# Sparse attention of a hybrid decoder block: a unit's transposes first, then its value products in one row from the last tile, with eight transposed tiles in one ring

## The chip, the cores and the metric

The kernel runs on one core of a Trainium2 chip. The metric is the device time of one execution in microseconds (us). Five engines of the core work side by side, each through its own instructions in a fixed order: TensorE (PE in the profile; PEld are its weight loads), VectorE (DVE), ScalarE (ACT), GpSimd (POOL), and SyncE (SP), which here issues all DMAs. Matrix results land in PSUM, eight banks of 512 float32 columns on 128 partitions; ScalarE and VectorE copy from there to SBUF.

## What is computed

One decoder block on 1024 tokens of width 1024: RMS norm, one input projection, two groups of attention heads side by side, a gated sum, an output projection and the residual. The reference, cut to the parts that the change touches and their neighbours:

```python
o_diff = diff_attention(dq, dk, dv, lam, diff_slopes)          # 4 heads, two softmaxes each
o_cmp, p_cmp = compressed_attention(nq, kc, vc)                # 63 compressed keys
sel_idx = select_blocks(p_cmp)                                 # top 8 blocks of 64 keys
o_slc = selected_attention(nq, k_slc, nkv[3], sel_idx, nsa_slopes)
o_win = window_attention(nq, k_win, nkv[5], nsa_slopes)        # band of 512 keys
o_nsa = g[0] * o_cmp + g[1] * o_slc + g[2] * o_win
o_nsa = o_nsa.transpose(0, 3, 1, 2, 4).reshape(B, T, NSA_WIDTH) * jax.nn.silu(nz)
x = x + jnp.concatenate([o_diff, o_nsa], axis=-1) @ w_out[layer]
```

The sparse group has 8 query heads on 2 key/value heads of width 64. Everything is float32; the scores and projections use a high and a low part of their operands in float32r.

## The kernel before

Three stages follow each other. **Stage 1** makes all projections, and writes queries, keys, values and gates to DRAM. **Stage 2** is the sparse attention. It goes over eight q tiles of 128 tokens (`qt`). In each it takes branch 1 (window, at most five key tiles) and branch 0 (selected, up to `qt + 1` key tiles, the choice of blocks done as a mask), and in each branch two head pairs `gp`. One such piece, q tile by branch by `gp`, is a *unit*: 32 units in all. A unit's scores and softmax are `nsa_softmax` (which calls `softmax_pair`: scores on PE at L439, mask and row minimum on DVE at L443, exponential on ACT at L445; then POOL scales the rows at L585, in tiles called P or Pw). Its second half is `nsa_values` (L604): for each key tile, four transposes of 128x128 into one PSUM tile Tp (L611), a copy of Tp to the SBUF tile pT (`evac`: two of three on ACT at L489, the third on DVE at L487), and two value products (L615) that read pT and the values vsw and add into the accumulator O, one for each key/value head, each with 64 output columns. The products of float32 operands show as two records each, so that one key tile has four L615 records. There are 132 key tiles over all units.

Around it, in each q tile: the compressed branch of the *next* q tile (`cmp_branch`: products L516, DVE work from L519 on), its transposed weights pcT (copy L656, product L658 which starts O), and the output projection of the *previous* q tile (`out_proj`, L475 to L477, 24 matmuls of 512 columns). **Stage 3** is the differential attention, q tiles from 7 down to 0, four heads each; its transposes are at L733, its copies use the same `evac`, its value products are at L737. It reads the keys of heads 0 and 1 from dkA and of heads 2 and 3 from dkB, and the values from dv, which it loads at its beginning (L690).

What sets the order: the kernel is written for a scheduler that places each engine's instructions by its own model of time; the written order gives dependencies and priority, not the final sequence. Two PSUM tiles serve all transposes (`psT`, 2 buffers). pT has four buffers in a pool that lives for stages 2 and 3; pcT has one buffer of its own. The weights of the output projection are loaded in eight pieces `wraw` (two DMAs each in stage 2) through two buffers, and split by ACT (L461) and DVE (L463 in stage 2) into woh and wol before their first use.

Of the kernel before, what the change touches and what calls it, by code (L numbers as in the profile page):

```python
# [8 lines left out]
F32 = mybir.dt.float32  # L9
# [18 lines left out]
def block_kernel(ctx: ExitStack, tc: tile.TileContext, x, norm_g, w_in, dq_g, dk_g, lq1, lk1, lq2, lk2,  # L28
                 sub_g, nq_g, nk_g, cmp_pos, cmp_w1, cmp_b1, cmp_w2, w_out, out):
    nc = tc.nc  # L30
# [18 lines left out]
    def T_tile():  # L49
        return psT.tile([128, 512], F32, tag="T", name="Tp")  # L50

    def A_tile():
        return psA.tile([128, 512], F32, tag="A", name="A")


    ident = const.tile([128, 128], F32, name="ident")
# [107 lines left out]
    with ExitStack() as p1:  # L164
# [5 lines left out]
        st = ctxS.enter_context(tc.tile_pool(name="p1s", bufs=2))  # L170
# [73 lines left out]
        with ExitStack() as pc:  # L244
# [5 lines left out]
            for tt in range(NT):  # L250
# [8 lines left out]
                raw = st.tile([128, 512], F32, tag="qn", name="kvraw", bufs=3)  # L259
# [135 lines left out]
        sh = ctx.enter_context(tc.tile_pool(name="attn", bufs=2, side="right"))  # L395
# [48 lines left out]
                                               scalar=3e38, op0=ALU.add, op1=ALU.min, accum_out=nm)  # L444
                nc.scalar.activation(Ps[a][:, :n], Ps[a][:, :n], AF.Exp, scale=-1.0, bias=nm, accum_out=ssums[a])  # L445

        def load_w_out(pool, raws, k0):

            woh = pool.tile([128, 4, 1024], F32R, name="woh")
            wol = pool.tile([128, 4, 1024], F32R, name="wol")  # L450
            for k in range(4):
                for nh in range(2):
                    c = slice(512 * nh, 512 * nh + 512)
                    raw = raws.tile([128, 512], F32, tag="wraw", name="wraw", bufs=2)
                    if k0 == 0:
                        nc.sync.dma_start(raw, w_out[128 * k:128 * k + 128, c])
                    else:
                        for j in range(2):
                            r0 = 512 + 256 * j + 64 * k
                            nc.sync.dma_start(raw[64 * j:64 * j + 64], w_out[r0:r0 + 64, c])  # L460
                    nc.scalar.activation(woh[:, k, c], raw, AF.Copy)  # L461
                    eng = nc.vector if k0 else nc.gpsimd
                    eng.tensor_tensor(wol[:, k, c], raw, woh[:, k, c].bitcast(F32), op=ALU.subtract)  # L463
            return woh, wol
# [16 lines left out]
        evac_n = [0]  # L481

        def evac(Tp, n=512, every=3):
            pT = sh.tile([128, 512], F32, tag="pT", name="pT", bufs=4)
            evac_n[0] += 1
            if evac_n[0] % every == 0:
                nc.vector.tensor_copy(pT[:, :n], Tp[:, :n])  # L487
            else:
                nc.scalar.activation(pT[:, :n], Tp[:, :n], AF.Copy)  # L489
            return pT  # L490
# [65 lines left out]
        def nsa_span(qt, br):  # L556
            k0 = max(0, qt - 4) if br == 1 else 0
            return k0, 128 * (qt + 1 - k0)
# [44 lines left out]

        def nsa_values(qt, br, gp, Ps, O):  # L604
            k0, n = nsa_span(qt, br)
            for kt in range(n // 128):
                Tp = T_tile()
                for j in range(2):
                    for g2 in range(2):
                        c = 256 * j + 128 * g2  # L610
                        nc.tensor.transpose(Tp[:, c:c + 128], Ps[g2, j][:, 128 * kt:128 * kt + 128], ident)  # L611
                pT = evac(Tp, 512, 3)
                last = br == 0 and gp == 1 and kt == n // 128 - 1
                for j in range(2):
                    nc.tensor.matmul(O[64 * j:64 * j + 64, 256 * gp:256 * gp + 256],  # L615
                                     vsw[:, br, k0 + kt, 64 * j:64 * j + 64], pT[:, 256 * j:256 * j + 256],
                                     start=False, stop=last)

        q_first = q_stack(q_d["nq"][0])
        for m in (2, 3, 0, 1):  # L620
# [2 lines left out]
        pools, early = {}, {}  # L623
# [16 lines left out]

    with ExitStack() as p2:
        pools["w"] = p2.enter_context(tc.tile_pool(name="p2w", bufs=1))
        keep = p2.enter_context(tc.tile_pool(name="p2k", bufs=1))
        st = p2.enter_context(tc.tile_pool(name="p2s", bufs=2))
        vsw = keep.tile([128, 2, NT, 128], F32, name="vsw")
        nc.sync.dma_start(vsw, v_d)
        wo_n = load_w_out(keep, st, 4)
        pending = None
        for qt in range(NT):
            t0 = 128 * qt  # L650
            QH, QL, nzt, gate, pg, rep = nxt
            Tp = A_tile()
            for g in range(4):
                nc.tensor.transpose(Tp[:, 128 * g:128 * g + 128], pg[:, g].rearrange("p k c -> p (k c)"), ident)
            pT = pools["w"].tile([128, 512], F32, tag="pcT", name="pcT", bufs=1)
            nc.scalar.activation(pT, Tp, AF.Copy)  # L656
            O = A_tile()
            nc.tensor.matmul(O, vcbd, pT, start=True, stop=False)  # L658
            if qt + 1 < NT:
                nxt = cmp_branch(qt + 1)  # L660


            for br in (1, 0):
                for gp in range(2):
                    Ps = early.pop((qt, br, gp), None) or nsa_softmax(qt, br, gp, QH, QL, gate, rep)
                    nsa_values(qt, br, gp, Ps, O)
            if pending:
                out_proj(*pending)
            nc.vector.tensor_tensor(nzt, O.rearrange("p (g q) -> p g q", g=4), nzt, op=ALU.mult)
            ch = st.tile([128, 4, 128], F32R, tag="ch", name="ch")  # L670
            cl = st.tile([128, 4, 128], F32R, tag="cl", name="cl")
            nc.scalar.activation(ch, nzt, AF.Copy)
            nc.gpsimd.tensor_tensor(cl, nzt, ch.bitcast(F32), op=ALU.subtract)
            pending = (st, ch, cl, wo_n, x[t0:t0 + 128], xa_d[qt], 1)
        O_first = A_tile()
        out_proj(*pending)
# [4 lines left out]
    with ExitStack() as p3:  # L681
        kp = p3.enter_context(tc.tile_pool(name="p3k", bufs=1))
        p2p = p3.enter_context(tc.tile_pool(name="p3p", bufs=1))
        big = p3.enter_context(tc.tile_pool(name="p3big", bufs=1))
        st = p3.enter_context(tc.tile_pool(name="p3s", bufs=1))
        right = p3.enter_context(tc.tile_pool(name="p3r", bufs=1, side="right"))
# [4 lines left out]
        for m in range(4):  # L691
            k_load(dkB[:, m], "dk", 4 + m)
        wo_d = load_w_out(big, st, 0)

        def loads(qt):
# [16 lines left out]
        for i, qt in enumerate(order):  # L712
            t0 = 128 * qt
            n = t0 + 128
# [3 lines left out]
            O = A_tile() if i else O_first  # L718
            for h in range(4):
# [9 lines left out]
                for k4 in range(0, qt + 1, 4):  # L729
                    kn = min(4, qt + 1 - k4)  # L730
                    Tp = T_tile()
                    for k in range(kn):
                        nc.tensor.transpose(Tp[:, 128 * k:128 * k + 128], P0[:, 128 * (k4 + k):128 * (k4 + k) + 128], ident)  # L733
                    pT = evac(Tp, 128 * kn, 4 if qt > 4 else 2)
                    for k in range(kn):
                        kt = k4 + k
# [40 lines left out]
```

## Time and profile before

| | us |
|---|---|
| median of three runs (range) | 832.72 (831.93 to 833.76) |
| the profiled execution | 832.81 |
| its span, first to last instruction | 831.1 |
| PE busy in the span | 795.2 (96%) |
| DVE, ACT, POOL busy | 511.4, 368.4, 357.3 |
| first transpose of stage 2 (L611) | 399.8 |
| last value product of stage 2 (L615) starts | 686.0 |

The page gives busy times over the whole span; a window gives the same for a stretch. A timeline shows instructions in order of time, equal neighbours merged into one row with a count. The end of a matmul is a model, its start is not, so distances between starts are what a price of a matmul is read from. PEclk is the share of the full TensorE clock that was granted.

### The profile page before, as it was taken

How to read it: one execution, taken by the hardware profiler on the slowest of the kernel's cores; microseconds unless marked ns; L12 is line 12 of the kernel's file. 1: busy time of each engine (PE TensorE's matmuls, PEld its weight loads, DVE VectorE, ACT ScalarE, POOL GpSimd, SP SyncE). 2: the span in 40 equal slices, each digit the busy share in tenths (PEclk: the TensorE clock that was granted, in tenths of full speed). 3: DMA queues.
4: the chain of work that ended last, by engine and by line, in shares of the span. 5: the costliest groups of instructions: out<-in, count | busy, mean ns of one | idle time of the engine just before them, and what ended most of it. 6: DMA issues, size and time to landing. Idle time of an engine off the chain costs nothing.

```text
span 831.1 us, 12884 instructions
## 1 busy us (share of the span) xinstructions
PE 795.2 (96%) x4457; PEld 631.1 (76%) x4457; DVE 511.4 (62%) x1183; ACT 368.4 (44%) x811; POOL 357.3 (43%) x385
## 2 busy tenths in 40 slices
PE   5999799999999999999899999999999999998997
PEld 4898688888888888888666666666665658888975
DVE  4644643368634439932697577776775267989743
ACT  6543131231323232012686656564656365867510
POOL 6734262250625434040476526263443314876421
PEclk9999999999999999999999999999999999999999
DMA  8637463151434423166543232121120426533233
GB/s 283 175 75 228 124 211 107 25 154 49 140 101 119 123 44 97 50 175 167 178 115 102 77 103 74 55 64 51 50 66 1 117 63 192 164 93 111 65 127 114
DMA packets 74897, 91.99 MB, mean 111 GB/s; under 512 B 14032, under 2 KB 48976, under 8 KB 74704
## 3 DMA queue, kind: packets, MB, share of 16 engines
q1 hardware_dynamic: 74832, 91.18, 37.7%
q8 instruction: 35, 0.57, 0.3%
q14 instruction: 30, 0.25, 0.1%
HBM read 63.89 MB, written 27.26 MB: 110 GB/s over the span
## 4 chain that ended last, share of the span: by engine, by line
PE 79%; DMA 7%; DVE 6%; POOL 2%; issue 2%; ACT 2%; SPq 2%; POOLq 0%; ACTq 0%; DVEq 0%
PE S L439 10%; PE A L615 9%; PE Tp L611 9%; PE A L208 5%; PE S L210 5%; PE A L210 5%; PE A L209 5%; PE S L209 5%; PE S L208 5%; PE A L475 3%; PE A L477 3%; PE A L476 3%; PE A L737 3%; PE Tp L152 2%; DMA xt<-in_x_dram 1%
## 5 line engine op out<-in xcount | busy, mean ns | idle before, releaser
L445 ACT ACTIVATE P<-P,nm 128x128 f32<-128x128 f32 (+7 forms) x136 | 101.2, 747 | 32.9 <-DVE nm L443 29.6
L489 ACT ACTIVATE pT<-Tp 128x512 f32<-128x512 f32 (+3 forms) x118 | 67.3, 575 | 90.8 <-PE Tp L611 72.1
L135 POOL TENSOR_TENSOR r<-ss,neghalf 128x8 f32<-128x8 f32 (+2 forms) x41 | 55.9, 1364 | 119.6 <-DVE ss L133 114.6
L200 POOL TENSOR_TENSOR wlo<-raw,whi 128x512 fp32r<-128x512 f32 (+2 forms) x64 | 82.4, 1315 | 50.8 <-ACT whi L199 49.3
L208 PE MATMUL A<-whi,xh 128*128 128x512 f32 (+2 forms) x224 | 86.6, 386 | 0.0
L208 PE MATMUL S<-whi,xh 128*128 128x512 f32 (+2 forms) x224 | 86.3, 385 | 0.3 <-ACT xh L240 0.2
L210 PE MATMUL S<-whi,xl 128*128 128x512 f32 (+2 forms) x224 | 86.5, 386 | 0.0
L209 PE MATMUL S<-wlo,xh 128*128 128x512 f32 (+2 forms) x224 | 86.1, 385 | 0.0
L210 PE MATMUL A<-whi,xl 128*128 128x512 f32 (+2 forms) x224 | 85.8, 383 | 0.0
L209 PE MATMUL A<-wlo,xh 128*128 128x512 f32 (+2 forms) x224 | 85.7, 383 | 0.0
L615 PE MATMUL A<-pT,vsw 128*64 128x256 f32 x528 | 84.7, 404 | 0.8 <-DMA vsw<-v_d 0.8
L585 POOL TENSOR_SCALAR P<-P,ssum 128x128 f32<-128x128 f32 (+7 forms) x72 | 51.5, 736 | 49.5 <-DVE ssum L581 20.3
L443 DVE CUSTOM_DVE_ANT_0 P<-S,D 128x128 f32<-128x128 f32 (+7 forms) x96 | 60.7, 659 | 18.1 <-PE S L439 12.0
L439 PE MATMUL S<-nsaK,QH 128*128 128x384 f32 (+2 forms) x192 | 68.9, 366 | 2.2 <-DVE nm L443 2.2
L585 POOL TENSOR_SCALAR Pw<-Pw,ssum 128x640 f32<-128x640 f32 (+3 forms) x56 | 39.1, 718 | 61.4 <-DVE ssum L581 37.1
L439 PE MATMUL S<-nsaK,QL 128*128 128x384 f32 (+2 forms) x192 | 61.4, 334 | 0.0
L160 DVE RECIPROCAL e<-e 128x512 f32<-128x512 f32 (+1 forms) x18 | 57.1, 3174 | 0.6
L487 DVE COPY pT<-Tp 128x512 f32<-128x512 f32 (+3 forms) x62 | 38.4, 619 | 30.5 <-PE Tp L611 28.9
L475 PE MATMUL A<-woh,ch 128*128 128x512 f32 x128 | 52.3, 409 | 4.3 <-ACT ch L705 3.3
L199 ACT ACTIVATE whi<-raw 128x512 fp32r<-128x512 f32 (+2 forms) x64 | 36.3, 605 | 43.2 <-DMA raw<-in_w_in_dram 37.2
L415 POOL TENSOR_TENSOR QL<-q,QH 128x1024 fp32r<-128x1024 f32 x16 | 39.0, 2438 | 31.8 <-ACT QH L414 24.0
L611 PEld LDWEIGHTS Tp<-ident,P 128*128 128x128 f32 x296 | 31.7, 142 | 26.8 <-issue 26.5
(185 smaller groups left out, 1819.3 us busy)
## 6 DMA issues: line engine op xcount, KB each, us to landing
raw<-in_w_in_dram SPq DMA_DIRECT2D x48, 256.0 KB, 3.0
xt<-in_x_dram SPq DMA_DIRECT2D x16, 512.0 KB, 3.5
w<-in_cmp_w_dram SPq DMA_DIRECT2D x16, 256.0 KB, 3.6
q<-nq_d SPq DMA_DIRECT2D x16, 256.0 KB, 4.1
xa_d<-xt SPq DMA_DIRECT2D x16, 256.0 KB, 2.0
q<-dq_d SPq DMA_DIRECT2D x16, 256.0 KB, 4.0
xt<-xa_d SPq DMA_DIRECT2D x8, 512.0 KB, 3.7
out_dram<-xt SPq DMA_DIRECT2D x16, 256.0 KB, 2.0
```

What stands on the lines that cost most here:

```text
L200: nc.gpsimd.tensor_tensor(l_, r_, h_.bitcast(F32), op=ALU.subtract)
L208: nc.tensor.matmul(A[:, :n], a, hi[:, k, :n], start=(k == 0), stop=False)
L209: nc.tensor.matmul(A[:, :n], a, lo[:, k, :n], start=False, stop=False)
L210: nc.tensor.matmul(A[:, :n], b, hi[:, k, :n], start=False, stop=(k == 7))
L439: nc.tensor.matmul(S[a][:, c0:c1], Q[:, heads[a]], Ks[a][:, w0 + c0 - o:w0 + c1 - o], start=Q is QH, stop=Q is QL)
L443: nc.vector.tensor_tensor_reduce(out=Ps[a][:, :n], in0=S[a][:, o:o + n], in1=biases[a], scale=-slopes[a], scalar=3e38, op0=ALU.add, op1=AL ...
L445: nc.scalar.activation(Ps[a][:, :n], Ps[a][:, :n], AF.Exp, scale=-1.0, bias=nm, accum_out=ssums[a])
L475: nc.tensor.matmul(A, ch[:, k], woh[:, k, c], start=(k == 0), stop=False)
L489: nc.scalar.activation(pT[:, :n], Tp[:, :n], AF.Copy)
L585: nc.gpsimd.tensor_scalar(P[:, :n], P[:, :n], ssum[:, g2, j:j + 1], 1.0, op0=ALU.mult, op1=ALU.mult)
L611: nc.tensor.transpose(Tp[:, c:c + 128], Ps[g2, j][:, 128 * kt:128 * kt + 128], ident)
L615: nc.tensor.matmul(O[64 * j:64 * j + 64, 256 * gp:256 * gp + 256], vsw[:, br, k0 + kt, 64 * j:64 * j + 64], pT[:, 256 * j:256 * j + 256], ...
```

## The change

`nsa_values` no longer goes from transposes to products tile by tile. It takes all key tiles of a unit (for more than five, in two parts of nearly equal size), emits all their transposes and copies, and then all their value products in one row, beginning with the tile that was copied last. So many copied tiles must be alive at once, so stage 2 gets one ring of eight 128x512 buffers named pT, and three users share it: the copies pT, the copy pcT, and the eight w_out pieces `wraw`, which come first. Stage 3 gets a ring of four pT in its own pool. The PSUM side stays at two tiles.

```diff
-        def load_w_out(pool, raws, k0):
+        def load_w_out(pool, raws, k0, tag="wraw", bufs=2):
...
-                    raw = raws.tile([128, 512], F32, tag="wraw", name="wraw", bufs=2)
+                    raw = raws.tile([128, 512], F32, tag=tag, name="wraw", bufs=bufs)
...
-            pT = sh.tile([128, 512], F32, tag="pT", name="pT", bufs=4)
+            pT = pools["pT"].tile([128, 512], F32, tag="pT", name="pT", bufs=pools["pT_bufs"])
...
-            for kt in range(n // 128):
-                Tp = T_tile()
-                for j in range(2):
-                    for g2 in range(2):
-                        c = 256 * j + 128 * g2
-                        nc.tensor.transpose(Tp[:, c:c + 128], Ps[g2, j][:, 128 * kt:128 * kt + 128], ident)
-                pT = evac(Tp, 512, 3)
-                last = br == 0 and gp == 1 and kt == n // 128 - 1
-                for j in range(2):
-                    nc.tensor.matmul(O[64 * j:64 * j + 64, 256 * gp:256 * gp + 256],
-                                     vsw[:, br, k0 + kt, 64 * j:64 * j + 64], pT[:, 256 * j:256 * j + 256],
-                                     start=False, stop=last)
+            nk = n // 128
+
+            first = 0
+            for size in ([nk] if nk <= 5 else [(nk + 1) // 2, nk // 2]):
+                pTs = []
+                for kt in range(first, first + size):
+                    Tp = T_tile()
+                    for j in range(2):
+                        for g2 in range(2):
+                            c = 256 * j + 128 * g2
+                            nc.tensor.transpose(Tp[:, c:c + 128], Ps[g2, j][:, 128 * kt:128 * kt + 128], ident)
+                    pTs.append((kt, evac(Tp, 512, 3)))
+                for kt, pT in reversed(pTs):
+                    last = br == 0 and gp == 1 and first + size == nk and kt == first
+                    for j in range(2):
+                        nc.tensor.matmul(O[64 * j:64 * j + 64, 256 * gp:256 * gp + 256],
+                                         vsw[:, br, k0 + kt, 64 * j:64 * j + 64], pT[:, 256 * j:256 * j + 256],
+                                         start=False, stop=last)
+                first += size
...
+        pools["pT"], pools["pT_bufs"] = pools["w"], 8
...
-        wo_n = load_w_out(keep, st, 4)
+        wo_n = load_w_out(keep, pools["pT"], 4, "pT", 8)
...
-            pT = pools["w"].tile([128, 512], F32, tag="pcT", name="pcT", bufs=1)
+            pT = pools["pT"].tile([128, 512], F32, tag="pT", name="pcT", bufs=8)
...
+        pools["pT"], pools["pT_bufs"] = p2p, 4
```

Behind the change the transposes stand at L616, the value products at L621, pcT's copy and product at L664 and L666, stage 3's transposes at L742, dv's load at L699, w_out and the projection at the old lines.

How the order of instructions moves, at three places. First PE in q tile 3, branch 1, before:

```order
L615 MATMUL A<-pT,vsw 64x256 x2
L611 MATMUL Tp<-ident,Pw 128x128 x4
L439 MATMUL S<-nsaK,QH 128x384
L439 MATMUL S<-nsaK,QL 128x384
L439 MATMUL S<-nsaK,QH 128x256
L439 MATMUL S<-nsaK,QL 128x256
L615 MATMUL A<-pT,vsw 64x256 x2
L611 MATMUL Tp<-ident,Pw 128x128 x4
L516 MATMUL A<-kcbd,qp 128x128 x4
```

and PE at the same place behind the change:

```order
L439 MATMUL S<-nsaK,QH 128x256
L439 MATMUL S<-nsaK,QL 128x256
L616 MATMUL Tp<-ident,Pw 128x128 x4
L516 MATMUL A<-kcbd,qp 128x128 x4
L616 MATMUL Tp<-ident,Pw 128x128 x8
L621 MATMUL A<-pT,vsw 64x256 x8
L616 MATMUL Tp<-ident,Pw 128x128 x4
L475 MATMUL A<-woh,ch 128x512
```

Before, every key tile's two products stand alone between transposes; now the eight products of a unit's four tiles are one row, with two tiles' transposes (the last of this unit, the first of the next) right ahead of them.

Second PE in the last q tile, branch 0, where no scores of stage 2 are left, before:

```order
L615 MATMUL A<-pT,vsw 64x256 x2
L611 MATMUL Tp<-ident,Pw 128x128 x4
L615 MATMUL A<-pT,vsw 64x256 x2
L611 MATMUL Tp<-ident,P 128x128 x4
L615 MATMUL A<-pT,vsw 64x256 x2
```

and behind the change:

```order
L616 MATMUL Tp<-ident,Pw 128x128 x8
L616 MATMUL Tp<-ident,P 128x128 x4
L621 MATMUL A<-pT,vsw 64x256 x10
L616 MATMUL Tp<-ident,P 128x128 x16
L621 MATMUL A<-pT,vsw 64x256 x8
L616 MATMUL Tp<-ident,P 128x128 x16
L621 MATMUL A<-pT,vsw 64x256 x8
L616 MATMUL Tp<-ident,P 128x128 x4
L439 MATMUL S<-dkA,QH 128x512
```

The strict change of one tile's transposes with one tile's products becomes runs of three and four tiles' transposes, with the row of a whole unit between.

Third SP, at the end of stage 2, the difference (- before, + behind the change; dkB are stage 3's keys in eight half loads, dv its values, xa_d the stores of the projection's partial result):

```order
 L421 DMA dkB<-dkl_d 64x1024 x2
 L421 DMA dkB<-dkh_d 64x1024 x2
+L699 DMA dv<-dv_d 128x512 x8
+L479 DMA xa_d<-xt 128x512
 L421 DMA dkB<-dkl_d 64x1024 x2
 L421 DMA dkB<-dkh_d 64x1024
-L411 DMA q<-dq_d 64x1024 x2
-L690 DMA dv<-dv_d 128x512 x8
-L479 DMA xa_d<-xt 128x512 x2
+L479 DMA xa_d<-xt 128x512
```

All eight half loads of dkB stood ahead of dv; now three of them stand behind dv and a store.

## Rows read from the trace of the kernel before

**Rows 1.** Page: the chain that ended last, its shares of the span by engine.

```profile
PE 79%; DMA 7%; DVE 6%; POOL 2%; issue 2%; ACT 2%; SPq 2%; POOLq 0%; ACTq 0%; DVEq 0%
```

**Rows 2.** Busy time of each engine by stretch, with granted clock.

```profile
core 0: us, PE busy (x) PEld busy (x) DVE busy (x) ACT busy (x) POOL busy (x), PEclk, DMA share, GB/s
400.00:420.00 20.00, 17.01 (x108) 13.25 (x107) 16.49 (x82) 17.25 (x57) 10.69 (x18) 0.91 0.60 186
420.00:440.00 20.00, 18.12 (x110) 12.27 (x108) 18.40 (x69) 16.19 (x45) 13.67 (x20) 1.00 0.42 107
...
500.00:520.00 20.00, 20.00 (x130) 14.08 (x129) 15.35 (x48) 12.83 (x27) 13.77 (x14) 1.00 0.29 79
...
680.00:690.00 10.00, 10.00 (x62) 6.75 (x61) 8.67 (x16) 7.90 (x15) 4.10 (x3) 1.00 0.06 14
```

**Rows 3.** Waits of PE alone, 455 to 690 us: the header, no entry under it.

```profile
engine line waited for: us in total, times, longest us
```

**Rows 4.** Timeline of PE, 502.7 to 504.3 us (start, duration, engine, line, tiles, count).

```profile
502.67 0.28 PE L439 MATMUL S<-nsaK,QH 128*128 128x256 f32 x1
502.79 0.28 PE L439 MATMUL S<-nsaK,QL 128*128 128x256 f32 x1
503.00 0.65 PE L615 MATMUL A<-pT,vsw 128*64 128x256 f32 x4
503.58 0.66 PE L611 MATMUL Tp<-ident,P 128*128 128x128 f32 x4
503.99 0.43 PE L439 MATMUL S<-nsaK,QH 128*128 128x384 f32 x1
```

**Rows 5.** Timeline of PE: a row of two tiles; transposes behind an ordinary matmul.

```profile
609.24 1.08 PE L615 MATMUL A<-pT,vsw 128*64 128x256 f32 x8
610.25 0.66 PE L611 MATMUL Tp<-ident,Pw 128*128 128x128 f32 x4
...
399.58 0.39 PE L210 MATMUL S<-whi,xl 128*128 128x512 f32 x1
399.81 0.60 PE L611 MATMUL Tp<-ident,P 128*128 128x128 f32 x4
400.17 0.37 PE L439 MATMUL S<-nsaK,QH 128*128 128x256 f32 x1
```

**Rows 6.** Tile pT: value products of stage 2, min/median/max ns, first and last start.

```profile
L615 PE MATMUL A<-pT,vsw x528: 379/379/689, 405.3 to 686.0; 128*64 128x256 f32 x176
```

**Rows 7.** Timeline at 661 us: a tile's transposes and copy; VectorE's copies by form.

```profile
661.13 0.66 PE L611 MATMUL Tp<-ident,P 128*128 128x128 f32 x4
...
661.82 0.60 ACT L489 ACTIVATE pT<-Tp 128x512 f32<-128x512 f32 x1 [1.68 <-PE Tp L611]
...
L487 DVE COPY pT<-Tp 128x512 f32<-128x512 f32 x38 | 26.1, 687 | 30.1 <-PE Tp L611 28.9 <-ACT Pw L445 1.0 <-issue 0.2
```

**Rows 8.** Tile wraw: issue and VectorE's split; timeline of VectorE at 405 us.

```profile
L460 SPq DMA_DIRECT2D wraw<-in_w_out_dram x16: 465/587/1679, 406.0 to 431.8; - x16
L463 DVE TENSOR_TENSOR wol<-wraw,woh x8: 675/718/2196, 412.1 to 438.3; 128x512 fp32r<-128x512 f32 x8
...
405.66 2.88 DVE L523 TENSOR_TENSOR u<-u,cnm 128x512 f32<-128x512 f32 x1
```

**Rows 9.** Timeline of PE, 409 to 412 us: an idle time, score steps after it.

```profile
409.36 0.39 PE L439 MATMUL S<-nsaK,QH 128*128 128x256 f32 x1 [1.83 <-DVE nm L443]
...
411.86 0.42 PE L439 MATMUL S<-nsaK,QH 128*128 128x256 f32 x1
412.08 0.42 PE L439 MATMUL S<-nsaK,QL 128*128 128x256 f32 x1
```

**Rows 10.** Timeline of SP at the end of stage 2; tile dkB.

```profile
663.80 0.60 SPq L421 DMA_DIRECT2D dkB<-dkh_d  x1
...
691.98 3.65 SPq L690 DMA_DIRECT2D dv<-dv_d  x8
...
DMA to landing us min/median/max: 5.3/7.1/8.5
```

## The prediction

> **What bounds the kernel now.** I read the page first, then the windows of 20 us, then single stretches in order of time. The page puts 79% of the chain that ended last on TensorE [rows 1]; its three largest lines are the scores (L439), the value products (L615) and the transposes (L611), the sparse stage's own work. The windows say where: from 460 to 680 us TensorE is busy for 20.00 of every 20 us (one of these eleven windows is shown), there with VectorE at 15.4 and ScalarE at 12.8 [rows 2]. Ends of matmuls are modelled, so I don't take the 20.00 for proof; the starts are. In order of time each group on PE starts a fixed step after the one before it, and PE's own list of waits from 455 to 690 us is empty [rows 3]. In this stretch the time is the sum of PE's steps. Before it, from 400 to 440 us, PE idles 4.9 us and VectorE is nearly full (16.5 and 18.4 of 20) [rows 2]. After the last value product, at 686.0 us [rows 6], the differential stage follows; VectorE is busy for 8.7 of 10 us at the change-over [rows 2].
>
> **What the change removes.** The price of a step depends on what stands beside it [rows 4, 5]. A row of value products works on 64 columns of the array (128\*64), everything else on 128.
> - Into a row: the step from a 256-column score matmul to the next is 0.12 us, and into the value products 0.21: 0.09 more.
> - A row of one tile (4 records): 0.58 us from its start to the transposes. A row of two tiles (8 records): 1.01. A second tile in the row costs 0.43.
> - Out of it: four transposes behind value products take 0.41 us to the next score matmul, behind an ordinary matmul 0.36: 0.05 more.
>
> So a tile with a row of its own costs 0.09 + 0.58 + 0.05 = 0.72 us, a tile inside a row 0.43: joining saves **0.29 to 0.30 us**. The order counts 124 rows before (116 of one tile, 8 of two, 132 tiles) and 40 behind the change (9 of five tiles, 11 of four, 10 of three, 3 of two, 7 of one). 84 rows fewer x 0.30 = **25.2 us**. The transposes that now follow scores pay nothing extra (0.36 above). The bounds are 84 x 0.28 = 23.5 and 84 x 0.31 = 26.0, by the rounding of the rows. No instruction is added or removed otherwise.
>
> **What it adds, first: waits for copies.** A unit's value products start with the tile that was copied last, so nothing of the row can run before that copy ends. From the first transpose of a tile to the start of its copy are 0.69 us, and the copy takes 0.60 on ScalarE or 0.69 on VectorE [rows 7]; 0.41 to 0.44 of that is the tile's own transposes. PE needs 0.87 to 0.97 us of other work between a tile's transposes and the product that reads it; the same holds between a tile and the next but one, since there are still two PSUM tiles for transposes. Before, the next tile's transposes and another tile's products always stood between (0.44 + 0.72). I laid the steps of [rows 4, 5] along the new order. Mostly scores or projections of 1 us and more stand between. In 10 of the 40 rows only one tile's transposes do (0.44): 10 x 0.48 = 4.8 us. In 8 places, nearly all in the last q tile where no scores are left (the runs of 12 and 16 transposes), a third tile in a row finds its PSUM tile still being copied: 8 x 0.43 = 3.4. I take **+8 us**. Lower bound 5, the ten rows alone; upper bound 16, if each of the other 30 rows waits 0.27 more, the half of a copy, since ScalarE is busy for 12.8 of 20 us [rows 2] and its copies then stand behind exponentials. I stay near the lower bound, since copies stood behind exponentials before as well, and PE waited for none of them [rows 3].
>
> Here a rule speaks against the change. The rows show the copy at 0.60 to 0.69 us against 0.44 for four transposes [rows 7]. The Trainium skill (Perfetto Trace Analysis, Matmuls) says that independent groups should rotate through PSUM banks so that the evacuation of one overlaps the matmuls of the next. Transposes in one row with two banks are short of such matmuls; by that rule the first rival below would come true, at 841 us and not 820.6, and what speaks for my smaller term are the scores that the order puts between most transposes.
>
> **Second: the start of the sparse stage.** The eight w_out loads now go through the ring of eight in which pT and pcT live. The first pcT, and all of PE's work behind its product, must wait until w_out's first tile is split on both engines; in ScalarE's order this pcT stands behind five w_out conversions and eight exponentials, before it stood ahead of all. A conversion takes 0.72 us on VectorE, and a load 0.59 to issue (16 of them, 9.4 us) [rows 8]. From 400 us on that is past 409, and VectorE waits for loads in a stretch in which it did the compressed branch's L523 (2.88 us) before [rows 8]. Its total work until 440 us is unchanged, so only that hole is lost: **+3 us**. Lower bound -2: PE idles 4.9 us from 400 to 440 [rows 2], and the part of it that waited for late w_out pieces goes away. Upper bound +8: eight VectorE conversions in front (5.8 us), and a slow clock. Before, after PE had stood 1.83 us at 407.5, score steps went from 0.12 to 0.22 us around 412, and the granted clock was 0.91 of full in 400 to 420 us [rows 2, 9]: some 4 us at the 1.2 GHz level, worth 2 us, which a longer hole would bring again.
>
> **Third: the hand-over.** The loads of the second half of the differential keys (dkB) were all issued by 664.4 us, long before the sparse stage's end [rows 6, 10]. In the new order SP holds the last three of the eight behind the eight dv loads, which waited for the last cl of the sparse stage (L690, issued from 691.98) [rows 10]. Queued behind them: one xa_d store, then w_out's second half. Two of four heads' scores move behind the last value product, with their softmax on a VectorE that is busy 8.7 of 10 us there [rows 2]. PE covers with 24 projection matmuls at 0.23 us (5.5 us) [rows 5]. dv's issue (3.65 us) and a landing of 7.1 [rows 10] are longer than this cover by 5.2: upper bound +5. Lower bound 0, no gain, since the same work only comes later. I take **+2**, because value products of the first two heads stand in that gap too.
>
> **The sum.** The profiled execution took 832.8 us (span 831.1, 1.7 around it), the median of the runs 832.7: the same. 832.8 - 25.2 + 8 + 3 + 2 = **820.6 us**. Best ends together: 832.8 - 26 + 5 - 2 - 0 = 810; all worst ends: 832.8 - 23.5 + 16 + 8 + 5 = 838.
>
> **The rivals.**
> 1. *Copies set the pace, slower than before.* In place of the switch PE waits at the end of each row. It decides from 25.2 - 5 (start and hand-over) = 20.2 us over 40 rows: **0.5 us of waiting per row**. With two PSUM tiles and nothing between, two tiles take 0.69 + 0.60 = 1.29 us or 0.65 each against 0.44: 132 x 0.21 = 28 us, time 832.8 - 25.2 + 28 + 5 = 841. For it: the last q tile's order is just that, and ScalarE is 60% full. Against it: 101 separate groups of transposes are left, and scores or projections follow most. Chance 0.08.
> 2. *The switch price is not real*: the modelled records show 0.72, but the stage follows VectorE or ScalarE, and the time stays at 831.5 to 834.3. For it: busy time on PE is modelled [rows 2]. Against it: starts are not modelled, and VectorE has a quarter of its time free. Chance 0.03.
> 3. *Start and hand-over take most*: +8 and +5 with waits of 12: 832.8 - 25.2 + 25 = 832.6. Two queues must go wrong together. Chance 0.05, split between no change and slightly faster.
> 4. *No waits*: 832.8 - 26 = 807 to 810. Against it: the ten rows with 0.44 us of cover. Chance 0.06.
>
> **How the numbers follow.** The forecast, a saving that is mostly kept (811 to 829), has 0.78. The range of 8 in 10 is 810 to 830: it leaves out rival 1, rival 2 and the far ends of 3 and 4. A measurement of this kernel can tell about 0.2% (1.7 us) from no change. Faster: forecast, rival 4 and part of 3, 0.87; within 0.2%: rival 2 and part of 3, 0.05; slower: rival 1, 0.08.
>
> **What the new profile would show.** Right: 40 runs of value products in PE's starts, the tile inside a row 0.43 us after the one before it; from 460 us on PE still busy for 20 of 20 us; the last value product some 15 us earlier than 686.0; idle times of PE that end with pT's copy (ScalarE or VectorE) in the last q tile, 0.3 to 0.6 us each. The start: PE idle for several us before 415 with pcT as releaser, and the first value products later than 405.3 [rows 6]. The hand-over: scores from dkB only behind the first projection matmuls. Wrong: idle times ended by pT's copy of over 0.5 us on most rows all along (rival 1); a row of five tiles that takes as long as five rows (rival 2); a clock below full in the windows after 440 us; a last value product that is 15 us earlier and a differential stage that is longer by as much.

## The result, and the profile after

The changed kernel takes **842.95 us** (median of four runs, 840.09 to 847.44) against 832.44 before (four runs): ratio 1.0129, 95% interval 1.0081 to 1.0176. It is 10.5 us slower; I had forecast 820.6 and a range of 810 to 830. The profiled execution of after has a span of 842.0 us, 10.9 more than before.

Where the time went is read in four views. First, the value products of stage 2 in the tile view of pT; columns as in [rows 6]:

```profile
L621 PE MATMUL A<-pT,vsw x528: 378/380/690, 419.2 to 678.4; 128*64 128x256 f32 x176
```

The first starts 13.9 us later than before, the last 7.6 earlier, and from there to the end of the span it takes 163.6 us instead of 145.1. So the sparse stage did become shorter, by 21.4 us between its first and last value product, and the loss lies at its two ends: 13.9 at the start, 18.5 behind it. (These three are not the prices yet. Before, 16 score matmuls of stage 3 on dkB stood ahead of the last value product, and now none does; a part of the 18.5 is that work, moved.)

The windows that answer to [rows 2]:

```profile
core 0: us, PE busy (x) PEld busy (x) DVE busy (x) ACT busy (x) POOL busy (x), PEclk, DMA share, GB/s
400.00:420.00 20.00, 10.96 (x57) 7.87 (x55) 13.26 (x57) 14.05 (x45) 10.16 (x17) 0.77 0.78 224
420.00:440.00 20.00, 17.01 (x87) 11.44 (x86) 14.52 (x65) 11.19 (x32) 10.51 (x15) 0.81 0.25 67
500.00:520.00 20.00, 20.00 (x152) 17.39 (x151) 15.23 (x50) 16.13 (x35) 10.14 (x12) 1.00 0.17 56
680.00:690.00 10.00, 7.46 (x25) 5.77 (x26) 1.92 (x3) 1.43 (x3) 1.29 (x1) 0.83 1.02 273
```

At 500 us TensorE is as full as before, and starts 152 matmuls instead of 130. From 400 to 440 it is busy for 28 of 40 us instead of 35.1, at a granted clock of 0.77 and 0.81. From 680 to 690 VectorE is busy for 1.9 of 10 us, where it had 8.7.

PE's waits from 455 to 690 us; this list was empty before [rows 3]:

```profile
engine line waited for: us in total, times, longest us
PE S L439 <- DMA dkB<-dkl_d: 2.3, 1, 2.3
PE A L621 <- ACT pT L489: 2.0, 5, 0.8
PE Tp L616 <- DVE pT L487: 1.7, 2, 1.2
PE A L621 <- DVE pT L487: 1.6, 2, 1.2
PE Tp L616 <- ACT pT L489: 1.3, 5, 0.3
PE A L475 <- ACT ch L680: 0.9, 1, 0.9
...
```

The four lines with pT are the waits for copies that I had priced: 6.6 us in 14 places. The first line is new: TensorE waits for a load of dkB. (The three lines left out are 1.7 us together.)

Last, what the DMA queue itself waited for: of each list the line on dkB's loads (L421), first of the kernel before, then of after, 640 to 690 and 640 to 700 us (the columns of [rows 3]):

```profile
SPq L421 <- PE Tp L611: 0.4, 1, 0.4
```

```profile
SPq L421 <- PE A L621: 22.4, 1, 22.4
```

This is the row that decides the case. A load of dkB (L421) has no operand that TensorE makes. It waited for TensorE all the same: before, for 0.4 us, for the transposes at L611; after, for 22.4 us, for the value products. The only thing that a load can wait for there is the memory it writes: whoever read these bytes last must be done. The compiled programs say which bytes (KB of each partition of SBUF):

| | Pw | ring pT | bs | vsw | dkB | P2 (stage 3) |
|---|---|---|---|---|---|---|
| before | 41 to 61 | 216 to 224 | 61 to 69 | 69 to 77 | 39 to 55 | 55 to 83 |
| after | 55 to 75 | **39 to 55** | 75 to 83 | 83 to 91 | **39 to 55** | 63 to 91 |

Before, dkB took the place of pcT and Pw, and its first load goes out right behind the last transposes that read them:

```profile
658.79 0.66 PE L611 MATMUL Tp<-ident,Pw 128*128 128x128 f32 x4
...
659.47 0.45 SPq L421 DMA_DIRECT2D dkB<-dkh_d  x1
```

After, the ring of eight is the first thing allocated in stage 2, and dkB lies exactly on it. The ring is read until the very last value product, so all eight loads wait for it, and SP's order puts dv's eight between them. The compiled programs have the same waits on the first load: before on a transpose of Pw, after on a value product that reads the ring.

```profile
656.11 0.33 SPq L470 DMA_DIRECT2D xt<-in_x_dram  x1
678.86 0.45 SPq L421 DMA_DIRECT2D dkB<-dkh_d  x1
...
681.91 5.59 SPq L699 DMA_DIRECT2D dv<-dv_d  x8
689.52 0.32 SPq L479 DMA_DIRECT2D xa_d<-xt  x1
689.89 1.76 SPq L421 DMA_DIRECT2D dkB<-dkl_d  x2
```

What it costs is seen on VectorE in stage 3 (one window of before, then two of after):

```profile
680.00:700.00 20.00, 19.35 (x109) 14.26 (x108) 17.55 (x28) 11.65 (x21) 8.22 (x6) 1.00 0.45 143
...
680.00:700.00 20.00, 16.96 (x89) 13.97 (x89) 7.42 (x12) 5.08 (x9) 2.48 (x2) 0.91 0.87 239
740.00:760.00 20.00, 19.20 (x127) 17.55 (x127) 19.84 (x48) 13.61 (x31) 10.48 (x9) 1.00 0.41 119
```

Between 680 and 700 us VectorE has no scores to mask and works for 7.4 of 20 us, where it had 17.55. From 740 to 760 it is full (19.84 of 20), so it can't make the hole good there.

The start, PE and then ScalarE of after, in order of time:

```profile
409.32 0.28 PE L439 MATMUL S<-nsaK,QL 128*128 128x256 f32 x1
415.49 2.07 PE L666 MATMUL A<-pcT,vcbd 128*128 128x512 f32 x2 [5.89 <-ACT pcT L664]
```

```profile
411.73 0.63 ACT L461 ACTIVATE woh<-wraw 128x512 fp32r<-128x512 f32 x1 [1.43 <-DMA wraw<-in_w_out_dram]
413.49 0.63 ACT L461 ACTIVATE woh<-wraw 128x512 fp32r<-128x512 f32 x1 [1.13 <-DMA wraw<-in_w_out_dram]
414.32 0.63 ACT L461 ACTIVATE woh<-wraw 128x512 fp32r<-128x512 f32 x1 [0.21 <-DMA wraw<-in_w_out_dram]
414.86 0.58 ACT L664 ACTIVATE pcT<-A 128x512 f32<-128x512 f32 x1
```

The order that the prediction described is there: pcT behind five conversions. But ScalarE stands for 2.8 us ahead of the last three, since w_out's loads are late, and TensorE stands for 5.89 us. Its clock is then at the lower of its two levels, 1.2 GHz (0.50 of full):

```profile
412.00:416.00 4.00, 0.51 (x1) 0.50 (x2) 2.45 (x3) 2.66 (x6) 4.00 (x6) 0.50 0.62 174
416.00:420.00 4.00, 4.00 (x14) 2.24 (x12) 2.68 (x12) 1.97 (x4) 0.07 (x1) 0.50 0.81 239
```

### The profile page after: what moved, and what is told of

It is laid out like the page before. It is cut to its first block, busy times and chain, and to the rows that moved or that the text cites. A ratio compares the mean times of both kernels' runs of the same rounds, so it can differ in the third digit from the quotient of the medians.

```text
span 842.0 us, 12838 instructions
## 1 busy us (share of the span) xinstructions
PE 782.1 (93%) x4457; PEld 644.2 (77%) x4457; DVE 514.8 (61%) x1183; ACT 368.1 (44%) x811; POOL 359.7 (43%) x385
## 5 line engine op out<-in xcount | busy, mean ns | idle before, releaser
L135 POOL TENSOR_TENSOR r<-ss,neghalf 128x8 f32<-128x8 f32 (+2 forms) x41 | 54.2, 1322 | 120.6 <-DVE ss L133 116.9
L621 PE MATMUL A<-pT,vsw 128*64 128x256 f32 x528 | 66.8, 391 | 3.7 <-ACT pT L489 2.0
L585 POOL TENSOR_SCALAR Pw<-Pw,ssum 128x640 f32<-128x640 f32 (+3 forms) x56 | 43.0, 788 | 46.5 <-DVE ssum L581 34.0
L621 PEld LDWEIGHTS A<-pT,vsw 128*64 128x64 f32 x528 | 34.5, 137 | 25.7 <-issue 4.1
L735 POOL TENSOR_SCALAR P<-P,dsum,neglam 128x1024 f32<-128x1024 f32 (+7 forms) x32 | 30.0, 937 | 53.3 <-DVE dsum L734 33.0
```

Of the source, the lines that this page charges most:

```text
L585: nc.gpsimd.tensor_scalar(P[:, :n], P[:, :n], ssum[:, g2, j:j + 1], 1.0, op0=ALU.mult, op1=ALU.mult)
```

## The experiments

Three things can be set apart by where a pool is opened, without a change to what is computed: the place of the ring, the place of w_out's pieces, and the order of the value products. Each kernel was timed beside the kernel before on the same chip; that one's median was between 832.25 and 834.23, and only in e12 above 832.9. Differences below are of the medians; each kernel has four to ten runs, and a difference of two is sure to some 2 to 3 us, those that involve after's four scattered runs to 4 or 5.

| | ring of pT | w_out's pieces | value products | us | ratio to before (95%) |
|---|---|---|---|---|---|
| after | 8, ahead of Pw | in the ring | rows | 842.95 | 1.0129 (1.0081 to 1.0176) |
| e1 | 8, at the end of stage 2 | in the ring | rows | 832.67 | 1.0002 (0.9986 to 1.0018) |
| e2 | 6, ahead of Pw | own two buffers | rows | 834.51 | 1.0020 (1.0005 to 1.0035) |
| e3 | 6, at the end | own | rows | 828.05 | 0.9938 (0.9916 to 0.9959) |
| e4 | 8, ahead of Pw | in the ring | tile by tile | 859.34 | 1.0314 (1.0287 to 1.0340) |
| e5 | 8, behind bs | in the ring | rows | 828.72 | 0.9945 (0.9928 to 0.9962) |
| e6 | 6, behind bs | own | rows | 820.32 | 0.9836 (0.9807 to 0.9865) |
| e7 | as e6 | own | first tile first | 835.11 | 1.0030 (1.0016 to 1.0043) |
| e8 | as e6 | own | tile by tile | 838.14 | 1.0058 (1.0039 to 1.0077) |
| e9 | the kernel before, vsw ahead of Pw | own | tile by tile | 838.42 | 1.0076 (1.0061 to 1.0091) |
| e10 | as e5 | in the ring, later | rows | 822.00 | 0.9883 (0.9866 to 0.9899) |
| e11 | as e6, stage 3's ring last | own | rows | **816.20** | 0.9813 (0.9797 to 0.9828) |
| e12 | as after, stage 3's ring last | in the ring | rows | 836.95 | 1.0044 (1.0023 to 1.0064) |
| e13 | as e11, but ahead of Pw | own | rows | 826.53 | 0.9923 (0.9900 to 0.9947) |
| e14 | as e11 | own | tile by tile | 833.87 | 1.0016 (0.9997 to 1.0035) |
| e15 | as e13 | own | tile by tile | 839.59 | 1.0079 (1.0052 to 1.0106) |

### Undoing one end at a time: e1 to e4

e1, the ring in a pool of its own behind all others of stage 2:

```diff
-        pools["pT"], pools["pT_bufs"] = pools["w"], 8
...
         st = p2.enter_context(tc.tile_pool(name="p2s", bufs=2))
+        pools["pT"], pools["pT_bufs"] = p2.enter_context(tc.tile_pool(name="p2r", bufs=1)), 8
```

> The changed kernel, but the ring of eight pT buffers lies in a pool of its own at the end of stage 2's memory, so that dkB, which takes the first 16 KB of that memory in stage 3, no longer lies on the ring; the start with its eight w_out pieces in the ring stays. Theory A (the hand-over costs 18 us, since dkB's loads have to wait for the last value product): dkB's first load before 665 us instead of 678.9, time 825 (821 to 830). Rival B (the hand-over is late because VectorE and ScalarE carry more late work in the new order of products): dkB loads early, but the time stays at 838 to 845.

dkB's loads start at 656.6 us again, and 10.3 us come back: less than theory A expected, much more than B allows. The first value product, though, was now at 422.2 us, 3 later than in after: at the end of stage 2's memory (119 to 135 KB) the ring lies on stage 1's small buffers. That these are still in use is read from the places, not shown by a wait; what is shown is that the next place (e5) doesn't have it.

e2, w_out's pieces in their own two buffers (the ring then has room for six):

```diff
-        pools["pT"], pools["pT_bufs"] = pools["w"], 8
+        pools["pT"], pools["pT_bufs"] = pools["w"], 6
...
-        wo_n = load_w_out(keep, pools["pT"], 4, "pT", 8)
+        wo_n = load_w_out(keep, st, 4)
...
```

> The changed kernel, but w_out's pieces have their own two buffers again and the ring has six (eight do not fit beside them); the ring stays where dkB will lie. Theory A (the start costs 14 us, since the first pcT waits in ScalarE's order behind five conversions that wait for DMAs): first value products at 405 instead of 419, time 829 (826 to 833), the hand-over still late. Rival B (the start is late because all transposes of a unit come first): first value products stay at 415 or later, time 838 to 845.

The start is as before, to 0.4 us, and 8.4 us come back; I had expected 14.

```profile
L621 PE MATMUL A<-pT,vsw x528: 379/379/431, 404.9 to 667.1; 128*64 128x256 f32 x176
```

So the 13.9 us by which the first value product was late are not the price of the start. While these waited, TensorE did scores that it has to do anyway.

e3 has both edits:

> The changed kernel with both: ring of six in a pool of its own at the end of stage 2's memory, w_out's pieces in their own two buffers. Theory A (two separate losses of 14 and 18 us around a gain of 17 to 21): 814 (810 to 818). Rival B (copies set the pace of the middle, and a ring of six is too small): 828 or more, with idle times of TensorE that end with pT's copy on most rows.

A miss for both theories in number: 828.05. The first value product is at 411.3 us, not at 405, which is e1's bad place again; and stage 3 was longer than I thought (below, e11).

e4 keeps after's memory and undoes the rows, with the old loop of `nsa_values`:

> The changed kernel's memory (one ring of eight for pT, pcT and w_out's pieces, lying where dkB will lie), but the value products tile by tile as before the change. Theory A (memory alone makes the loss, the row of products makes the gain): 832.7 + 14 + 18 = 863 (856 to 868). Rival B (the rows of products upset the start and the hand-over): 830 to 836.

859.34: theory A, clearly. The rows of products are worth 16.4 us in the changed kernel, and its memory costs 27. B is out: without the rows both ends are lost all the same.

### The ring in a better place: e5 to e8

e5 opens the ring's pool right behind the pool of Pw and bs, so dkB lies on Pw, and the ring doesn't lie on stage 1's late buffers:

```diff
-        pools["pT"], pools["pT_bufs"] = pools["w"], 8
+        pools["pT"], pools["pT_bufs"] = p2.enter_context(tc.tile_pool(name="p2r", bufs=1)), 8
```

> The changed kernel, but the ring of eight lies behind Pw and bs in stage 2's memory instead of ahead of them (67 to 83 KB instead of 39 to 55), so dkB (39 to 55 KB) lies on Pw as before the change; the start is left as the change made it. Theory A (dkB waits for whoever last read its memory): dkB's first load before 662 us, the start still 14 us late, time 827 (823 to 831). Rival B (the hand-over is late because of the new order of products): 838 to 845.

```profile
L421 SPq DMA_DIRECT2D dkB<-dkh_d x4: 444/522/648, 653.6 to 658.4; - x4
```

828.72, 14.2 us faster than after by the place of one pool. e6 takes w_out's pieces out as well:

> The same place for the ring, six buffers, and w_out's pieces in their own two again. Theory A (two losses from memory, a gain of 17 to 20 us from the rows, and stage 3 giving back 3 to 6 us of it as in the last run of both): first value products at 405, last value product 19 us earlier than before the change, time 817 (813 to 821). Rival B (the last run's 828 is the floor, since VectorE sets the pace of stage 3): 825 to 829, with stage 3 as long as the last value product is early.

820.32. Theory A's 817 is met within its range, and e3's 828 was no floor. With both ends mended the first value product is at 406.2 us and the last at 671.3, 14.6 us earlier than before the change (I had expected 19). Both differences appear twice: the start is worth 8.4 us (after to e2, e5 to e6), the place of dkB 14.2 (after to e5, e2 to e6). They add up. (The 14.2 hold with P2 where the change put it; see e11 to e15.)

e7 starts a unit's products with the first tile, e8 puts them back tile by tile; the memory is e6's.

```diff
-                for kt, pT in reversed(pTs):
-                    last = br == 0 and gp == 1 and first + size == nk and kt == first
+                for kt, pT in pTs:
+                    last = br == 0 and gp == 1 and kt == nk - 1
```

> As the run before, but the value products of a unit in the order of the tiles instead of from the last: nothing forces them into one row, and the order of the program has 110 rows (88 of one tile, 21 of two, one of one and a half) instead of 39. Theory A (each row more costs 0.30 us, waits for the last copy of a row give 4 to 8 back): 15 us slower than the run before. Rival C (rows don't matter, the memory does): within 4 us of it.

> Memory as in the two runs before (ring of six behind Pw and bs, w_out's pieces apart), the value products tile by tile as before the change: 127 rows. Theory A: 18 us slower than with the rows from the last tile (15 to 22), so 835 (831 to 839), about the kernel before. Rival C: within 4 us of the rows from the last tile.

e7 is 14.8 us slower than e6 (15 expected), e8 17.8 (18 expected). C is out. Only the reversed order makes rows: in tile order the scheduler starts each product as soon as its copy is there, and 111 rows are left of e8's 127; e6 has 39. PE's waits from 455 to 670 us, first of e7 (an empty list, as in e8), then of e6:

```profile
engine line waited for: us in total, times, longest us
```

```profile
PE Tp L616 <- DVE pT L487: 1.7, 2, 1.2
PE Tp L616 <- ACT pT L489: 1.5, 5, 0.3
...
PE A L621 <- ACT pT L489: 0.8, 3, 0.3
...
PE A L621 <- DVE pT L487: 0.3, 1, 0.3
```

With short rows TensorE waits for no copy; with e6's it waits 4.3 us (and 1.8 us more in the two lines left out, for other tiles). From these follows the price of a row: e8 to e7, without waits on either side, 3.0 us for 16 rows, 0.19 each; e8 to e6, 17.8 us and the 4.3 of waiting for 88 rows, 0.25 each. The first is rough: by the scatter of the runs the 16 rows are worth 1 to 4 us.

### The late load by itself: e9

One edit to the kernel *before*: vsw, which every value product reads, is allocated ahead of Pw, and so under dkB.

```diff
+        vsw = p2.enter_context(tc.tile_pool(name="p2v", bufs=1)).tile([128, 2, NT, 128], F32, name="vsw")
         pools["w"] = p2.enter_context(tc.tile_pool(name="p2w", bufs=1))
...
-        vsw = keep.tile([128, 2, NT, 128], F32, name="vsw")
```

> The kernel before the change, its products tile by tile, with one edit: vsw, the values that every value product reads, lies ahead of Pw in stage 2's memory (39 to 47 KB), where dkB (39 to 55 KB) will lie. Theory A (dkB's loads wait for the last reader of their memory, and that alone is the late hand-over): the sparse stage as before, dkB's first load behind the last value product instead of at 659 us, time 849 (846 to 853), 16 us lost after 675 us. Rival B (the hand-over of the changed kernel was late for another reason): 831 to 835.

```profile
SPq L421 <- PE A L615: 22.7, 1, 22.7
```

The mechanism is the predicted one, to the row: the same wait of 22 us, the same split of dkB's loads around dv's in SP's order, an otherwise untouched kernel. The price is not: 5.9 us, not 16. Something made the late load dearer in the changed kernel.

### The start taken apart: e10

e10 is e5 with the call of `load_w_out` moved behind the first pcT, the pieces still in the ring:

> The changed kernel with the ring of eight behind Pw and bs, and w_out's pieces still in the ring, but loaded after the first pcT instead of ahead of it. Theory A (the start is late because the first pcT waits for a place in the ring, and stands in ScalarE's order behind five conversions that wait for loads): first value products before 408 us, time 818 (814 to 822). Rival D (eight pieces in a ring that pT needs are too many, wherever they stand): first value products late by 5 us or more, time 824 to 829.

822.00, at the end of A's range, though the first value product is as late as D said (417.9 us). The order is what matters, with 6.7 us (e5 to e10); sharing the ring costs 1.7 (e10 to e6), which the scatter doesn't tell from none. What e10 gains over e5 lies behind the first value product: from 420 to 440 us TensorE is busy for 20.0 us in e10, for 17.0 in e5. ScalarE of e10 shows the rest: the third conversion waits for its load, and the pT copies stand behind it.

```profile
413.22 0.63 ACT L461 ACTIVATE woh<-wraw 128x512 fp32r<-128x512 f32 x1 [3.24 <-DMA wraw<-in_w_out_dram]
...
417.28 1.05 ACT L489 ACTIVATE pT<-Tp 128x512 f32<-128x512 f32 x2
```

### Stage 3's memory: e11 and e12

The change also put stage 3's own ring of four into the pool of P2, ahead of it, which moves P2 from 55 to 63 KB (and with it w_out's second half and the small buffers behind it). e11 is e6 with that ring in a pool at the end of stage 3's memory; e12 is after with the same edit.

```diff
-        pools["pT"], pools["pT_bufs"] = p2p, 4
...
         st = p3.enter_context(tc.tile_pool(name="p3s", bufs=1))
+        pools["pT"], pools["pT_bufs"] = p3.enter_context(tc.tile_pool(name="p3t", bufs=1)), 4
```

> The fastest run so far (ring of six behind Pw and bs, w_out's pieces apart; 820.3) with stage 3's own ring of pT at the end of stage 3's memory, so that P2 lies at 55 to 83 KB as before the change and not on w_out's first half (87 to 91 KB), which the last projection of stage 2 reads. Theory E (the 3 to 4 us that stage 3 still loses between 705 and 720 us are P2 tiles that wait for that projection): 817 (815 to 819). Rival F (they come from the new order of stage 3's instructions): 819 to 822.

> The changed kernel with one edit: stage 3's own ring of pT lies at the end of stage 3's memory, so P2 lies at 55 to 83 KB as before the change, and no longer on vsw (83 to 91 KB); the ring of eight stays ahead of Pw, with w_out's pieces, and dkB on it. Theory E (of the 16 to 17 us lost at the hand-over some 4 are P2's place, as in the run before, 6 to 7 dkB's place, as in the old kernel with vsw first, and the rest the thinner cover): 838.5 (836.5 to 840.5). Theory G (as long as dkB is late nothing else matters): 841 to 845.

Both land with theory E: 4.1 us in e11, 6.0 in e12. **e11 is the fastest kernel of the study, 816.20 us, 1.9% faster than before.** What is shown is the price of this edit: the same step tile by tile is worth 4.3 (e8 to e14). By means instead of medians it is 3.1 in e11, where the single runs of the two kernels overlap; in e12 it is 7.8 if each kernel is set against the kernel before on its own chip. That the price is P2's, and not that of the other tiles that move with it, is not shown. Theory E's reason, that P2's tiles wait for the last projection of stage 2, can't be the reason in after, where P2 (63 to 91 KB) doesn't reach w_out's tiles (91 to 123 KB); no wait row names P2, and the scheduler orders stage 3 anew with the edit. Below, "P2's place" stands for the whole edit.

### Why the late load was dearer: e13 to e15

A small table of four: late dkB or not, rows or tile by tile, all with w_out's pieces apart and P2 in its old place. e13 and e15 open the ring's pool ahead of Pw's; e14 is e11 with the old loop.

> The fastest run so far (816.2: rows of products, ring of six behind Pw and bs, w_out's pieces apart, stage 3's ring at the end) with only the ring of six moved ahead of Pw, so that dkB lies on it again. dkB's place cost 14.2 us in the changed kernel and 5.9 in the old one. Theory H (the rows of products, with nothing else left to do behind the last of them, make the late dkB dearer): 830 (828 to 833). Theory I (P2's place makes it dearer, and here P2 lies as before the change): 822 (820 to 825).

> The memory of the fastest run, the products tile by tile as before the change. Theory A (17.8 us for the rows, as measured with P2 in the other place): 834 (832 to 836), which is the kernel before. A row's price that depends on stage 3: outside of it.

> Products tile by tile with the ring of six ahead of Pw, dkB on it, the rest as in the fastest run. Theories H and I both: 6 us above the run before, 840 (838 to 842), as in the old kernel with vsw first. More than 10 above it: the cost of a late dkB is neither a matter of the rows nor of P2.

| | dkB early | dkB late | cost of the late load |
|---|---|---|---|
| tile by tile | 833.87 (e14) | 839.59 (e15) | 5.7 (e9: 5.9) |
| rows | 816.20 (e11) | 826.53 (e13) | 10.3 |
| rows, P2 moved too | 820.32 (e6) | 834.51 (e2) | 14.2 |

826.53 lies between H and I, and both were half right: in this memory the rows make a late dkB 4.6 us dearer, P2's place 3.9 more. Read the other way, with dkB late the rows gain 13.1 us here (e15 to e13) and not 17.7. This doesn't carry over to every memory: with P2 moved and w_out's pieces in the ring, the start and the late load together cost 21.2 us tile by tile (e8 to e4) and 22.6 in rows (e6 to after), a difference of 1.4, which the scatter doesn't tell from none. A reason for the rows' part may be seen in PE's waits of e13 from 655 to 720 us:

```profile
...
PE A L746 <- DMA dv<-dv_d: 1.9, 4, 1.1
PE S L439 <- DMA dkB<-dkl_d: 1.8, 1, 1.8
...
PE A L621 <- ACT pT L489: 0.8, 1, 0.8
PE A L475 <- ACT ch L680: 0.8, 1, 0.8
...
```

Before the last row there are only transposes, their copies, and nothing else for TensorE to do: the scores of stage 3 that filled this place before can't run without dkB. In e15 the two last lines shown don't appear. They are 1.6 us of the 4.6; the rest is not traced to a wait.

## Why the prediction was wrong

**What bounds the kernel** was right for the kernel before: making TensorE's steps cheaper there gained 16.4 to 17.8 us in three pairs of kernels (next paragraph).

**The rows and the copies** were right as a sum. I took 25.2 off and put 8 on: 17.2. Measured are 16.4 (e4 to after), 17.8 (e8 to e6) and 17.7 (e14 to e11); 13.1 where dkB is late and P2 in its old place (e15 to e13). Both terms were a little too large: a row less is worth 0.19 to 0.25 us instead of 0.30, the waits for copies are 6.6 us instead of 8. The Trainium skill (TensorEngine Tiling (Array Packing), Key Properties) says that a change of the tiling mode drains TensorE. The runs fit that, with this price; that the drain is what costs, no run separates. The rule of the Trainium skill that I weighed (Perfetto Trace Analysis, Matmuls), to rotate PSUM banks so that copies hide behind other matmuls, has the right sign. Here it shows as 6.6 us of waits where there were none, against some 23 us (16.4 + 6.6) that the rows save ahead of these waits.

**The start** was mis-sized: +3 (at most 8) against 8.4. The step that failed is "only that hole is lost", with the price of a load behind it: I counted w_out's 16 loads by the 0.59 us that SP needs to issue one, and put their landing at nothing. The issue of one took what I had counted (median 0.594); the landing is what ScalarE waited for (tile wraw of after):

```profile
L460 SPq DMA_DIRECT2D wraw<-in_w_out_dram x16: 465/594/1542, 399.4 to 413.6; - x16
...
DMA to landing us min/median/max: 2.5/3.4/8.9
```

Before, the longest landing was 4.3 us. In after the loads come earlier, and a load of 1 MB, vsw, goes out among them at 403.15 us and takes 8.2 us to land. ScalarE's third conversion waits until 411.73 us for a load issued behind it. That vsw's load is what held the others up fits the order of landing and was not tested. So pcT came at 414.9 instead of 409. TensorE stood for 5.9 us, and its granted clock was 0.50 from 412 to 420 us, which I had put only into the upper bound.

**The hand-over** was the step that decided: +2 (0 to 5) against 14.2 (10.3 with P2 in its old place). I had read from SP's order that three of dkB's eight loads stand behind dv's, and priced these three. That all eight would start 19 us later I could not see there, since an order says nothing of what its first row waits for. I left the first five where the kernel before has them, from 659.5 us on, as if that start were dkB's own. The row that gives it away, a load that waits 0.4 us for transposes at L611, stood in the list of the queue's own waits of the kernel before, which I had in front of me; I built on PE's waits alone. Three loads behind dv were a sign of the late start (e9 has them too), not its cause.

**What was missing altogether** is P2's place, a term put at nothing without a reason: 4.1 us (e6 to e11), from eight kilobytes that the change's last line puts ahead of P2.

The terms as measured: 832.4 - 17.1 (the mean of 16.4 and 17.8) + 8.4 + 14.2 + 4.1 = 842.0, against 842.95. That it comes out is no proof of the split: the three losses are steps of one path from after by e2 and e6 to e11. On the path by e12 and e13 the same steps are P2 6.0, start 10.4, dkB 10.3 (7.8, 8.4 and 10.6 with each kernel set against the one before on its own chip). So the start is worth 8.4 either way, while dkB's place and P2's make each other dearer.

**The rivals.** Rival 1 named 841 us, close to the result, for a reason that did not occur, so that was luck: it needed 28 us of waiting for copies, and there are 6.6. Rival 3 had the right two places, and sizes of 8 and 5 for what became 8.4 and 14.2, with a chance of 0.05. Rival 2 is refuted by e8 and e14. The chance of 0.08 for slower was too small, since each of the two ends had been bounded only by what could be seen of its queue.

**The signs.** "PE idle for several us before 415 with pcT as releaser" came true; so did the 40 rows, and scores from dkB only behind the first projection matmuls. TensorE is not busy for all of every 20 us from 460 us on: 18.7 to 20.0 up to 660 us, 16.6 from 660 to 680. The last value product came 7.6 us earlier instead of 15 (in e6, without the two losses, 14.6). Two signs of a wrong forecast are there: a clock below full after 440 us (0.91 from 680 to 720), and "a differential stage that is longer by as much": the tail behind the last value product grew by 18.5 us.

## What to carry to other kernels

When a change moves a buffer to another pool, list whose bytes it will lie under later, and when its last reader ends: the next stage's loads inherit that time. The waits of the DMA queue show it before any run, as a load that waits for an engine that makes none of its operands. And the gain of the change itself, 13 to 18 us, was there all along: with both rings of pT in other places and w_out's pieces in their own buffers, the same rows of products take 816.2 us.

## What the runs showed of the hardware

- A row of products on 64 columns between matmuls on 128 costs some 0.19 to 0.25 us more than the same products inside a row (e8 to e7 and e6).
- Of TensorE's clock: behind a wait of 5.89 us it was granted 0.50, its lower level of 1.2 GHz, from 416 to 420 us. Behind waits of 0.87 and 2.30 us in after it was 0.61 in 684 to 688 us, part at the one level and part at the other:

```profile
684.00:688.00 4.00, 4.00 (x12) 3.16 (x12) 1.23 (x2) 0.85 (x1) 0.00 (x0) 0.61 1.03 259
```

- The same loads of w_out took SP as long to issue in either kernel (median 0.587 us before, 0.594 in after), and up to 8.9 us to land in after where 4.3 was the longest before; the DMA engines were busy for 0.78 of the 20 us from 400 in after, for 0.60 before.
